# A two-block transformer kernel on one core: dense products of the second block with 512 columns of activations per matmul instead of 256

## The chip, the core and the metric

The kernel runs on one core of a Trainium2 chip. The metric is the device time of one execution in microseconds (us): before the change, the median of three runs is 1532.46 us (1531.75 to 1533.73).

## What is computed

A sequence of 256 tokens of width 1024 passes through a first block (attention, mLSTM, a mixture of experts), which the change does not touch, and then through a second block of two layers. Each layer projects the normed input into several parts, mixes the sequence, attends to 256 memory rows, gates, and projects back. Cut to what matters here:

```python
def second_block(x, mem, ...):
    mem_n = rms_norm_2(mem, mem_norm_w)
    for i in range(2):
        h = rms_norm_2(x, norm_w[i])
        if i == 0:                                   # gated linear attention (GLA)
            q, k, v, r, z, xq = split_cols(h @ gla_w_in, [512, 512, 2048, 16, 3072, 1024])
            ...
        else:                                        # S5
            u, z, xq = split_cols(h @ s5_w_in, [2048, 3072, 1024])
            y = s5_chunked(u, ...) + d * u
            y = jax.nn.gelu(y)
            seq_out = y * jax.nn.sigmoid(y @ w_glu + b_glu)
        xa = memory_attention(xq, mem_n, xa_w_kv[i])  # 4 heads of 256
        y = jnp.concatenate([seq_out, xa], -1) * jax.nn.silu(z)
        x = x + y @ w_out[i]
    return rms_norm_2(x, final_norm_w)
```

## The kernel before

All weights and activations are float32. For the dense products every operand is split on the chip into a high part (rounded to the matmul type fp32r) and a low part (the rest): `split` (L265 to 269) does the high part on ScalarE (L267) and the low part on VectorE (L268), or on GpSimd. `halves` (L271) loads 1 MB of weights into a tile `w` of 128 x 2048 and yields two halves of 1024 columns, each as a pair `whi`, `wlo`. A product is then three matmuls, hi by hi, hi by lo and lo by hi (`mm3`, L282), all issued in `mm` (L280), each with 256 moving columns (the 256 tokens). `dense_t` (L288) makes 256 output features out of one `w`: 2 halves x 8 slices of the contraction x 3, which is 48 matmuls into one PSUM bank; VectorE then multiplies the bank by the row of inverse norms `r` as it copies it out.

Layer one is `gla` (L1395 to 1581). It runs, in the order of the code: `gqk` (4 `dense_t`: queries and keys), a 16-wide gate product, `gv` (values, `dense_n`, eight blocks of 256 columns, tokens as weights), the chunked attention core, then `gx` (4 `dense_t`: the queries of the memory attention, tile `hf`), `mem_attention` (L1141 to 1169), and a loop of 12 `gz` blocks (`dense_t`, evicted as `zt` at L1555, Silu, `gated`), each followed with one block's delay by `wout` (L1378), 48 matmuls into four accumulating banks `acc`. Into the `gz` loop the code writes 8 calls of `s5_out` (L1324, all on GpSimd, with a DMA store of `tab2` at L1343) and 8 of `s5_in` (L1363), which prepare tables for layer two: GpSimd issues two DMA loads (L1367 and L1368, tile `gv`, the second of them from `md`), VectorE does six operations (L1372 to 1374), GpSimd issues the DMA store (L1375). The tile `s_t2` is shared by both and has two buffers, so a table can be begun only when the store of the one before the last has landed. In the profile it is called `s_t`.

`mem_attention` handles four heads one after the other, each in two tiles of 128 queries: scores (tile `at` from `w` and `hf`), maximum (L1154, L1155), exponential (L1158), reciprocal and scaling (L1159, L1160), two transposes (L1162); at the end of a head a copy (L1163), the product with the values (`at` from `xpT` and `w`), and a copy into `hf` (L1168).

Layer two is `s5` (L1584 to 1796): `su` (8 blocks) and `sx` (4 blocks) with the state products between them, then `mem_attention` again, with 12 `z_block` (L1607, evicted at L1610) and a complex scan on VectorE (L1634 to 1637) between its steps, then the output tables, and last the GLU: 16 features `f`, each 48 matmuls from `in_sglu`, a Sigmoid on ScalarE, and `wout`.

The order of each engine's instructions is not that of the code: the tile framework moves instructions across blocks where data and buffers allow. What it cannot move across is a change of the PSUM pools. `psum_banks` (L222) releases the pool of PSUM banks and allocates another with other tags, and a tile of the new pool comes after the tiles of the old one. In `gla` the second pool is `acc=4, ps=2, at=2` banks: the memory attention (`at`), the `gz` blocks (`ps`) and `wout` (`acc`) have banks side by side.

Of the kernel before, what the change touches and what calls it, by code (L numbers as in the profile page):

```python
# [19 lines left out]
T = 256  # L20
# [68 lines left out]
def pack(inputs):  # L89
# [55 lines left out]
    a["gv"] = blocks(np.ascontiguousarray(w[:, 1024:3072]), 256)  # L145
# [62 lines left out]
class Kern:  # L208
# [13 lines left out]
    def psum_banks(self, **banks):  # L222

        if self.ps is not None:
            self.ps.release()
        assert sum(banks.values()) <= 8
# [4 lines left out]
    def psum(self, tag="ps"):  # L231
        return self.ps.tile([128, 512], F32, tag=tag, name=tag, bufs=self.banks[tag])
# [69 lines left out]

    def dense_n(self, src, act):
# [37 lines left out]
    def rows(self, pool, col, name=None):  # L341

        ps = self.psum()[:, :T]
        for t in range(2):
            self.mm(ps[:, 128 * t:128 * t + 128], col[:, t:t + 1].to_broadcast([128, 128]), self.ident, True, True)
        if name is None:
            return ps
        r = self.t(pool, [128, T], name)
        self.nc.scalar.activation(r, ps, AF.Copy)
        return r  # L350
# [1044 lines left out]
    def gla(self):  # L1395
        nc, io, tc = self.nc, self.io, self.tc
        G0 = self.G
        with tc.tile_pool(name="g", bufs=1) as P, tc.tile_pool(name="gw", bufs=2) as W, \
# [10 lines left out]
            hh = self.t(G0, [128, 8, T], "hh", F32R)  # L1409
            hl = self.t(G0, [128, 8, T], "hl", F32R)  # L1410
# [6 lines left out]
            h = (hh, hl)  # L1417
            first = self.dense_t(io["gqk"][0], h)
# [14 lines left out]
            for s in range(2):  # L1433
                o = self.t(P, [128, 4, T], "gqk%d" % s)
                for b in range(2):
                    ps = first if s + b == 0 else self.dense_t(io["gqk"][2 * s + b], h)
                    nc.vector.tensor_mul(o[:, 2 * b:2 * b + 2], ps, bc(r, 2))
                qk.append(o)
# [8 lines left out]
            for k in range(8):  # L1447
                self.mm3(ps, [x[:, k] for x in wrs], [x[:, k] for x in h], k == 0, k == 7)
# [36 lines left out]
            for b in range(8):  # L1485
                ps = self.dense_n(io["gv"][b], h)
                for t in range(2):
                    nc.scalar.activation(v[:, t, 256 * b:256 * b + 256], ps[:, t], AF.Copy, scale=rc[:, t:t + 1])
# [76 lines left out]
            hh = self.t(G0, [128, 8, T], "hh", F32R)  # L1565
            hl = self.t(G0, [128, 8, T], "hl", F32R)
            ps = self.psum("at")[:, :2].rearrange("p (t n) -> p t n", t=2)
# [10 lines left out]
            self.h = (hh, hl)  # L1578
            self.su0 = self.dense_t(io["su"][0], self.h)
# [4 lines left out]
    def s5(self, out):  # L1584
        nc, io, tc = self.nc, self.io, self.tc
        x3 = self.xT
        self.psum_banks(ps=2, st=3, at=3)
        with ExitStack() as S:
# [13 lines left out]
            with ExitStack() as S2:  # L1602
# [4 lines left out]
                def z_block(b):  # L1607
                    ps = self.dense_t(io["sz"][b], h)
                    zt = self.t(W, [128, 2, T], "zt")
                    nc.vector.tensor_mul(zt, ps, bc(r, 2))  # L1610
# [49 lines left out]
                with tc.tile_pool(name="su", bufs=1) as S1:  # L1660
# [47 lines left out]
                    for n in range(4):  # L1708
                        for b in (n, n + 4):
                            ps = self.dense_t(io["su"][b], h, st if 2 * n + b // 4 >= 3 else iter(())) if b else self.su0  # L1710
                            u = self.t(W, [128, 2, T], "zt")
                            nc.vector.tensor_mul(u, ps, bc(r, 2))
# [3 lines left out]
                    for b in range(4):  # L1716
                        ps = self.dense_t(io["sx"][b], h, st)
                        nc.vector.tensor_mul(xa[:, 2 * b:2 * b + 2], ps, bc(r, 2))
# [15 lines left out]
            ys = [[None] * 16, [None] * 16]  # L1734
            for jb in range(8):
# [11 lines left out]
                for par in range(2):  # L1747
# [4 lines left out]
                    for n in range(2):  # L1752
                        ys[n][f] = y2[:, n]
                    self.split(u, ys[0][f], ys[1][f])
# [9 lines left out]
            for f in (16, 17, 18, 19, 20, 21, 22, 23, 0, 1, 2, 3, 4, 5, 6, 7, 8, 9, 10, 11, 12, 13, 14, 15):  # L1764
# [6 lines left out]
                ps = self.psum()[:, :T]  # L1771
# [28 lines left out]
def tile_kernel(ctx: ExitStack, tc: tile.TileContext, io, out, dbg=None, upto=99):  # L1800
# [8 lines left out]
    if upto >= 3:  # L1809
        k.psum_banks(ps=8)  # L1810
# [27 lines left out]
```

## Time and profile before

| | |
|---|---|
| median of three runs | 1532.46 us |
| the profiled execution | 1531.12 us, span 1529.1 us, mean granted TensorE clock 0.919 |
| TensorE (PE) busy | 1349.4 us, 88% |
| VectorE (DVE) busy | 762.3 us, 50% |
| ScalarE (ACT) busy | 551.3 us, 36% |
| GpSimd (POOL) busy | 321.7 us, 21% |
| memory attention of layer one to the end of its `wout` | 910.42 to 1097.00 us |
| `su` and `sx` with the state products | 1112.60 to 1225.46 us |
| memory attention of layer two, z blocks, scan | 1225.46 to 1322.37 us |
| GLU and its `wout` | 1376.49 to 1514.74 us |

Times in the trace are microseconds from the start of the span. PE is busy for most of the span, so stretches in which it is not, and stretches in which another engine is full, are where to look. The granted clock is a share of TensorE's full 2.4 GHz; at 0.50 it is at its lower level of 1.2 GHz.

### The profile page before, as it was taken

The numbers are of one execution on the slowest core, as the hardware profiler recorded it, in microseconds if no ns is written. First come the engines' busy times: TensorE is split into PE (matmuls) and PEld (weight loads), VectorE is DVE, ScalarE is ACT, GpSimd is POOL, SyncE is SP. The second block draws the span as 40 slices with busy tenths as digits, with TensorE's granted clock in tenths as the row PEclk, the third lists the DMA queues.
The fourth block names the chain that finished last, engine by engine and source line by source line (L and its number), as shares of the span: only waits on it lengthen the run. The fifth ranks groups of instructions, "written<-read, shape, count | busy, mean of one in ns | idle before, by whom it ended". The sixth has DMA issues, their size and how long they took to land. (4 is left out here: it accounts for less than half of the span.)

```text
span 1529.1 us, 25802 instructions
## 1 busy us (share of the span) xinstructions
PE 1349.4 (88%) x10632; PEld 1072.4 (70%) x10632; DVE 762.3 (50%) x1498; ACT 551.3 (36%) x861; POOL 321.7 (21%) x450
## 2 busy tenths in 40 slices
PE   5999998888798889776698976899989998999997
PEld 2777896444454545311188976799988998999997
DVE  2766454721243300100177766756735899754553
ACT  3754552221211212110045423454522255444443
POOL 0041031321323231100059765100310000030001
PEclk8999999987898988887798996999989999999998
DMA  9776765999999999999974566755556535574540
GB/s 374 266 267 249 281 230 212 384 397 421 420 408 416 421 420 420 417 421 380 421 264 147 183 183 212 256 196 204 180 181 199 173 111 194 195 214 171 193 139 28
DMA packets 87626, 414.86 MB, mean 271 GB/s; under 512 B 26432, under 2 KB 28016, under 8 KB 43472
## 3 DMA queue, kind: packets, MB, share of 16 engines
q1 hardware_dynamic: 66768, 381.85, 65.7%
q0 software_dynamic: 8016, 22.13, 4.6%
q10 hardware_dynamic: 12720, 9.18, 1.8%
q8 instruction: 86, 1.41, 0.4%
q14 instruction: 36, 0.29, 0.1%
HBM read 392.90 MB, written 20.22 MB: 270 GB/s over the span
## 5 line engine op out<-in xcount | busy, mean ns | idle before, releaser
L267 ACT ACTIVATE whi<-w 128x1024 fp32r<-128x1024 f32 x252 | 263.6, 1055 | 330.4 <-PE ps L280 243.3
L268 DVE TENSOR_TENSOR wlo<-w,whi 128x1024 fp32r<-128x1024 f32 x222 | 275.7, 1245 | 156.8 <-ACT whi L267 156.3
L280 PE MATMUL ps<-hh,whi 128*128 128x256 f32 x928 | 274.3, 296 | 13.3 <-DVE zt L1610 5.0
L280 PE MATMUL ps<-hh,wlo 128*128 128x256 f32 x928 | 269.3, 290 | 5.2 <-DVE wlo L268 5.1
L280 PE MATMUL ps<-hl,whi 128*128 128x256 f32 x928 | 268.4, 289 | 0.9 <-DVE hl L1575 0.7
L280 PEld LDWEIGHTS ps<-hh,whi 128*128 128x128 f32 x928 | 180.7, 195 | 22.0 <-issue 8.7
L280 PEld LDWEIGHTS ps<-hh,wlo 128*128 128x128 f32 x928 | 180.3, 194 | 8.0 <-DVE wlo L268 6.0
L280 PEld LDWEIGHTS ps<-hl,whi 128*128 128x128 f32 x928 | 180.4, 194 | 2.0 <-DVE hl L1575 0.7
L280 PE MATMUL A<-w,xg 128*32 128x512 f32 x984 | 142.8, 681 | 31.1 <-DMA w<-in_w 30.2
L280 PE MATMUL acc<-gyh,whi 128*128 128x256 f32 x384 | 110.6, 288 | 4.0 <-ACT gyh L267 4.0
L280 PE MATMUL acc<-gyl,whi 128*128 128x256 f32 x384 | 111.1, 289 | 1.9 <-DVE gyl L268 1.9
L280 PE MATMUL acc<-gyh,wlo 128*128 128x256 f32 x384 | 109.9, 286 | 0.0
L268 POOL TENSOR_TENSOR wlo<-w,whi 128x1024 fp32r<-128x1024 f32 x30 | 70.7, 2371 | 167.5 <-ACT whi L267 167.4
L934 DVE SCALAR_TENSOR_TENSOR xT<-m,mod,xT 128x256 f32<-128x256 f32 x64 | 27.8, 479 | 140.8 <-PE m L280 140.8
L280 PEld LDWEIGHTS A<-w,xg 128*32 128x32 f32 x984 | 23.9, 114 | 102.1 <-DMA w<-in_w 72.7
L280 PE MATMUL A<-w,gT 128*32 128x512 f32 x512 | 75.4, 690 | 22.3 <-DMA w<-in_w 14.4
L280 PEld LDWEIGHTS acc<-gyh,whi 128*128 128x128 f32 x384 | 74.3, 193 | 4.4 <-ACT gyh L267 4.2
L280 PEld LDWEIGHTS acc<-gyl,whi 128*128 128x128 f32 x384 | 74.4, 194 | 3.1 <-DVE gyl L268 2.4
L280 PEld LDWEIGHTS acc<-gyh,wlo 128*128 128x128 f32 x384 | 74.9, 195 | 0.2 <-issue 0.2
L960 DVE TENSOR_TENSOR g<-g,A 128x512 f32<-128x512 f32 x8 | 5.5, 684 | 134.8 <-PE A L280 134.8
L1755 POOL TENSOR_TENSOR zs<-zs,yy 128x256 f32<-128x256 f32 x16 | 14.0, 893 | 241.3 <-DMA yy<-yd 241.2
L280 PE MATMUL ps<-wlo,hh 128*128 128x256 f32 x192 | 55.7, 290 | 4.6 <-DVE wlo L268 4.6
(585 smaller groups left out, 2768.6 us busy)
## 6 DMA issues: line engine op xcount, KB each, us to landing
w<-in_w SPq DMA_DIRECT2D x187, 1024.0 KB, 11.4
w<-in_wada SPq DMA_DIRECT2D x24, 1024.0 KB, 7.3
w<-in_wo SPq DMA_DIRECT2D x24, 1024.0 KB, 4.9
w<-in_sglu SPq DMA_DIRECT2D x16, 1024.0 KB, 5.0
w<-in_gz SPq DMA_DIRECT2D x12, 1024.0 KB, 5.2
w<-in_sz SPq DMA_DIRECT2D x12, 1024.0 KB, 4.8
w<-in_win SPq DMA_DIRECT2D x10, 1024.0 KB, 7.3
w<-in_xk SPq DMA_DIRECT2D x8, 1024.0 KB, 9.9
```

The lines of the kernel that those rows point to most:

```text
L267: self.nc.scalar.activation(hi, src, AF.Copy)
L268: (eng or self.nc.vector).tensor_sub(lo, src, hi.bitcast(F32))
L280: self.nc.tensor.matmul(ps, l, r, start=start, stop=stop, **kw)
L934: self.nc.vector.scalar_tensor_tensor(self.xT[:, f], pc[:, T * c:T * c + T], self.m(5)[:, f:f + 1], self.xT[:, f], op0=OP.mult, op1=OP.add)
L960: nc.vector.tensor_mul(g1, g1, p3)
L1755: nc.gpsimd.tensor_mul(zs[:, f], zs[:, f], u)
```

## The change

A new `dense_w` takes the place of `dense_t` in 44 blocks (`gqk` 4, `gx` 4, `gz` 12, `su` 8, `sx` 4, `sz` 12). The high and the low half of the activations lie in one tile `h` of `[128, 2, 8, T]`, and one matmul multiplies the high weights by both, 512 columns; a second one of 256 columns multiplies the low weights by the high half. That is 32 matmuls in place of 48. The result has two parts, so the PSUM tile `pd` has two banks; `whole` joins them: ScalarE copies the second part into a tile `lo`, VectorE adds it to the first (L326) and multiplies by `r` (L327), where one VectorE multiplication stood. The GLU does the same with `mm2`, with a ScalarE copy and a VectorE addition more for each feature. The values `gv` come in blocks of 512 columns: 192 matmuls of 512 in place of 384 of 256. The PSUM pools change with the two-bank tiles:

```diff
+    def mm2(self, ps, l, r, start, stop):
+        self.mm(ps, l[0], r, start, False, skip_group_check=True)
+        self.mm(ps[:, 0], l[1], r[:, 0], False, stop, skip_group_check=True)
+
+    def dense_w(self, src, act, other=iter(())):
+        ps = self.psum("pd")
+        for c, w in enumerate(self.halves(src)):
+            w = [x.rearrange("p (k m) -> p k m", k=8) for x in w]
+            for k in range(8):
+                self.mm2(ps[:, c], [x[:, k] for x in w], act[:, :, k], k == 0, k == 7)
...
+    def whole(self, W, dst, ps, r):
+        lo = self.t(W, [128, 2, T], "lo")
+        self.nc.scalar.activation(lo, ps[:, :, 1], AF.Copy)
+        self.nc.vector.tensor_add(dst, ps[:, :, 0], lo)
+        self.nc.vector.tensor_mul(dst, dst, bc(r, 2))
...
# gla
-            self.psum_banks(acc=4, ps=2, at=2)
+            self.psum_banks(pd=2, at=4)
             xa = self.t(P, [128, 8, T], "hf")
             for b in range(4):
-                ps = self.dense_t(io["gx"][b], h)
-                nc.vector.tensor_mul(xa[:, 2 * b:2 * b + 2], ps, bc(r, 2))
+                ps = self.dense_w(io["gx"][b], h)
+                self.whole(W, xa[:, 2 * b:2 * b + 2], ps, r)
             self.mem_attention(W, xa, self.load_kv(0), xa)
             self.out("xa0", xa)
+            self.psum_banks(pd=2, acc=4)
             acc = [self.psum("acc") for _ in range(4)]
             late = []
             for b in range(12):
-                ps = self.dense_t(io["gz"][b], h)
+                ps = self.dense_w(io["gz"][b], h)
...
                 zt = self.t(W, [128, 2, T], "zt")
-                nc.vector.tensor_mul(zt, ps, bc(r, 2))
+                self.whole(W, zt, ps, r)
...
-                u = self.t(G0, [128, T], "u", bufs=4)
+                u = self.t(G0, [128, T], "u", bufs=3)
...
# s5
-        self.psum_banks(ps=2, st=3, at=3)
+        self.psum_banks(pd=2, st=4)
...
                 V = S2.enter_context(tc.tile_pool(name="sv", bufs=2))
+                self.psum_banks(pd=2, at=4)
                 scan(SCAN_FIRST)
...
-                ps = self.psum()[:, :T]
+                ps = self.psum().rearrange("p (a t) -> p a t", a=2)
                 for j, wg in enumerate(self.halves(io["sglu"][f])):
                     for k in range(8):
-                        self.mm3(ps, [x[:, 128 * k:128 * k + 128] for x in wg], [x[8 * (k % 2) + 4 * j + k // 2] for x in ys],
-                                 j + k == 0, j + k == 8)
+                        self.mm2(ps, [x[:, 128 * k:128 * k + 128] for x in wg], ys[8 * (k % 2) + 4 * j + k // 2], j + k == 0, j + k == 8)
                 sg = self.t(W, [128, T], "sg")
-                nc.scalar.activation(sg, ps, AF.Sigmoid, bias=self.v("s5_b_glu_2", f))
+                nc.scalar.activation(sg, ps[:, 1], AF.Copy)
+                nc.vector.tensor_add(sg, ps[:, 0], sg)
+                nc.scalar.activation(sg, sg, AF.Sigmoid, bias=self.v("s5_b_glu_2", f))
```

Two pool switches are new: one in `gla` between `mem_attention` and the `gz` loop, one in `s5` ahead of the second `mem_attention`. The pool at the start of `gla` goes from `ps=8` to `ps=4, pd=2`.

The order of instructions on the engines moves with the pools. On PE, before, the first steps of layer one's memory attention stand like this (`at` is the attention; the `ps` row ahead of it ends the last `gx` block, those behind it are of the first `gz` block, 40 of them between the first scores and the first transposes):

```order
L280 MATMUL ps<-hh,wlo 128x256
L280 MATMUL at<-w,hf 128x256 x2
L280 MATMUL ps<-hh,whi 128x256
L280 MATMUL ps<-hl,whi 128x256
...
L1162 MATMUL at<-c_ident,xp 128x128 x2
L280 MATMUL at<-w,hf 128x256 x2
L280 MATMUL ps<-hh,wlo 128x256
```

On PE, after the change, at the same place (the first two rows are the end of the last `gx` block, the last two the start of the first `gz` block; between them stand four heads of five rows each, and nothing else):

```order
L283 MATMUL pd<-h,whi 128x512
L283 MATMUL pd<-h,wlo 128x256
L283 MATMUL at<-w,hf 128x256 x2
L1188 MATMUL at<-c_ident,xp 128x128 x2
L283 MATMUL at<-w,hf 128x256 x2
L1188 MATMUL at<-c_ident,xp 128x128 x2
L283 MATMUL at<-xpT,w 128x256 x4
...
L283 MATMUL pd<-h,whi 128x512
L283 MATMUL pd<-h,wlo 128x256
```

All `gz` and `wout` matmuls now stand behind the whole memory attention on PE; the first four `gz` blocks and three of the twelve `wout` stood among its steps before.

On DVE, after the change, the end of the same attention (L1398 to 1400 are `s5_in`, `s_t2` its table; L1180 to 1186 the attention's softmax of the last two query tiles; L271 the low half of a `gz` weight):

```order
L1398 TENSOR_TENSOR s_t_9247<-gv 128x8x64
L1399 TENSOR_TENSOR gA<-gv 128x512
L1400 TENSOR_TENSOR s_t_9247<-s_t_9247,gA 128x8x64
L1180 TENSOR_REDUCE xmx<-at 128x1
L1181 TENSOR_SCALAR xmx<-xmx 128x1
L1185 RECIPROCAL xsm<-xsm 128x1
L1186 TENSOR_SCALAR xp<-xp,xsm 128x256
L1180 TENSOR_REDUCE xmx<-at 128x1
L1181 TENSOR_SCALAR xmx<-xmx 128x1
L271 TENSOR_TENSOR wlo<-w,whi 128x1024 x2
L326 TENSOR_TENSOR zt<-pd,lo 128x512
L327 TENSOR_TENSOR zt<-zt,r 128x512
```

`s_t_9247` is the last of the eight `s5_in` tables: all eight stand ahead of the last two query tiles on DVE, as they did before.

On DVE in layer two, after the change, one z block among the scan (L1667 to 1670) and the second memory attention:

```order
L326 TENSOR_TENSOR zt<-pd,lo 128x512
L1667 TENSOR_TENSOR zs<-Xs,pw 128x448
L1668 TENSOR_TENSOR zs<-Xs,pw 128x448
L1669 TENSOR_TENSOR zs<-zs,Xs 128x448
L1185 RECIPROCAL xsm<-xsm 128x1
L327 TENSOR_TENSOR zt<-zt,r_9512 128x512
L1670 TENSOR_TENSOR Xs<-zs 128x2x7x32
```

Where one eviction stood (L1610 before), two operations stand now, with a scan step's operations between them.

## Rows read from the trace of the kernel before

**Rows 1.** The page's busy time of each engine over the whole span.

```profile
PE 1349.4 (88%) x10632; PEld 1072.4 (70%) x10632; DVE 762.3 (50%) x1498; ACT 551.3 (36%) x861; POOL 321.7 (21%) x450
```

**Rows 2.** Busy time by stretch: us, PE, PEld, DVE, ACT, POOL (instructions), clock, DMA, GB/s.

```profile
910.42:999.61 89.19, 67.02 (x418) 62.49 (x417) 58.28 (x105) 39.11 (x59) 33.62 (x63) 0.83 0.71 228
999.61:1097.00 97.39, 97.39 (x819) 97.39 (x817) 59.40 (x77) 48.19 (x64) 1.02 (x3) 1.00 0.58 197
1112.60:1225.46 112.86, 111.44 (x1296) 102.57 (x1297) 66.15 (x106) 26.68 (x29) 2.44 (x3) 0.96 0.59 184
1225.46:1322.37 96.91, 87.89 (x658) 83.95 (x656) 94.26 (x191) 53.94 (x70) 0.00 (x0) 0.98 0.44 154
1376.49:1514.74 138.25, 138.25 (x1155) 138.25 (x1154) 69.40 (x83) 61.50 (x82) 0.93 (x2) 1.00 0.40 138
```

**Rows 3.** The waits of 884 to 1000 us: engine, line, whom for; us, times, longest.

```profile
PE at L1162 <- DVE xp L1160: 13.4, 4, 7.2
DVE s_t L1372 <- DMA tab<-s_t: 10.2, 2, 8.5
DVE s_t L1372 <- DMA gv<-md: 8.2, 2, 6.1
DVE gA L1373 <- DMA gv<-md: 6.2, 2, 5.8
```

**Rows 4.** Timeline of POOL, 896 to 1000 us: start, us, what, and its idle time before.

```profile
942.30 0.59 POOL L1343 DMA_DIRECT2D tab<-s_t  x1 [0.30 <-POOL s_t L1341]
...
950.64 0.53 POOL L1375 DMA_DIRECT2D tab<-s_t  x1 [0.72 <-DVE s_t L1374]
...
968.28 0.53 POOL L1375 DMA_DIRECT2D tab<-s_t  x1 [0.19 <-issue]
...
989.13 0.53 POOL L1375 DMA_DIRECT2D tab<-s_t  x1 [7.55 <-DVE s_t L1374]
```

**Rows 5.** The tile md: its DMA loads at L1368, from issue to landing.

```profile
DMA to landing us min/median/max: 8.3/11.0/14.2
```

**Rows 6.** Two rows of DVE's timeline one behind the other, in the memory attention.

```profile
950.27 0.68 DVE L1555 TENSOR_TENSOR zt<-ps,r 128x512 f32<-128x512 f32 x1
950.87 0.68 DVE L1373 TENSOR_TENSOR gA<-gv 128x512 f32<-128x512 f32 x1
```

**Rows 7.** Timeline of the last query tile of layer one's memory attention, all engines.

```profile
990.88 1.03 PE L280 MATMUL at<-w,hf 128*128 128x256 f32 x4
...
992.79 0.42 DVE L1154 TENSOR_REDUCE xmx<-at 128x1 f32<-128x256 f32 x1
...
993.24 0.15 DVE L1155 TENSOR_SCALAR xmx<-xmx 128x1 f32<-128x1 f32 x1
...
994.88 0.48 ACT L1158 ACTIVATE xp<-at,xmx 128x256 f32<-128x256 f32 x1
995.25 0.19 ACT L1158 ACTIVATION_READ_ACCUMULATOR xp<-at,xmx 128x1 f32 x1
...
995.67 0.35 DVE L1160 TENSOR_SCALAR xp<-xp,xsm 128x256 f32<-128x256 f32 x1
...
996.90 0.58 ACT L1163 ACTIVATE xpT<-at 128x512 f32<-128x512 f32 x1
...
997.56 1.97 PE L280 MATMUL at<-xpT,w 128*128 128x256 f32 x8
```

**Rows 8.** The score matmuls' tile: duration in ns min/median/max, first and last start.

```profile
L280 PE MATMUL at<-w,hf x32: 377/379/635, 910.4 to 991.5; 128*128 128x256 f32 x32
```

**Rows 9.** Busy time in 40 us, one in the attention, one in the GLU.

```profile
920.00:960.00 40.00, 25.70 (x151) 23.76 (x149) 26.51 (x49) 17.00 (x26) 20.93 (x38) 0.74 0.68 216
...
1400.00:1440.00 40.00, 40.00 (x336) 40.00 (x335) 20.55 (x23) 17.31 (x23) 0.00 (x0) 1.00 0.47 162
```

**Rows 10.** DVE's groups by line in 1225.46 to 1322.37: busy us, mean ns, idle.

```profile
L1610 DVE TENSOR_TENSOR zt<-ps,r 128x512 f32<-128x512 f32 x12 | 8.1, 679 | 0.0
```

**Rows 11.** PE's waits in 1225.46 to 1322.37.

```profile
PE ps L280 <- DVE zt L1610: 5.0, 2, 2.7
```

More of the change, by code (lines that the diff above doesn't have):

```diff
@@ L144, in pack @@
     a["gqk"] = tcols(w[:, :1024])
-    a["gv"] = blocks(np.ascontiguousarray(w[:, 1024:3072]), 256)
+    a["gv"] = np.ascontiguousarray(w[:, 1024:3072].reshape(2, 4, 128, 4, 512).transpose(3, 0, 2, 1, 4))
     a["gr"] = blocks(np.ascontiguousarray(w[:, 3072:3088]), 16)
@@ L225, in psum_banks @@
             self.ps.release()
-        assert sum(banks.values()) <= 8
+        assert sum(n * (1 + (tag == "pd")) for tag, n in banks.items()) <= 8
         self.ps = self.tc.alloc_tile_pool(name="ps%d" % self.n, bufs=1, space=bass.MemoryType.PSUM)
@@ L231, in psum @@
     def psum(self, tag="ps"):
+        if tag == "pd":
+            return self.ps.tile([128, 2, 2, T], F32, tag=tag, name=tag, bufs=self.banks[tag])
         return self.ps.tile([128, 512], F32, tag=tag, name=tag, bufs=self.banks[tag])
@@ L301, in steps_t @@
                     yield
+    def mm2(self, ps, l, r, start, stop):
[7 more added lines that the diff above has]
+                self.mm2(ps[:, c], [x[:, k] for x in w], act[:, :, k], k == 0, k == 7)
+                if k % 4 == 3:
+                    next(other, None)
+        return ps
+    def whole(self, W, dst, ps, r):
[3 more added lines that the diff above has]
+        self.nc.vector.tensor_mul(dst, dst, bc(r, 2))
     def dense_n(self, src, act):
@@ L341, in rows @@
     def rows(self, pool, col, name=None):
-        ps = self.psum()[:, :T]
+        ps = (self.psum() if "ps" in self.banks else self.psum("acc"))[:, :T]
         for t in range(2):
@@ L1408, in gla @@
             self.root_table(W)
-            hh = self.t(G0, [128, 8, T], "hh", F32R)
-            hl = self.t(G0, [128, 8, T], "hl", F32R)
+            h = self.t(G0, [128, 2, 8, T], "h", F32R)
+            hh, hl = h[:, 0], h[:, 1]
             ps = self.psum()[:, :4].rearrange("p (t n) -> p t n", t=2)
@@ L1416, in gla @@
                 self.square_sums(G0, k, self.xT[:, k], mg[:, k], ps, bufs=3, eng=nc.vector)
-            h = (hh, hl)
-            first = self.dense_t(io["gqk"][0], h)
+            first = self.dense_w(io["gqk"][0], h)
             r12 = self.t(P, [128, 2, 2], "r12")
@@ L1435, in gla @@
                 for b in range(2):
-                    ps = first if s + b == 0 else self.dense_t(io["gqk"][2 * s + b], h)
-                    nc.vector.tensor_mul(o[:, 2 * b:2 * b + 2], ps, bc(r, 2))
+                    ps = first if s + b == 0 else self.dense_w(io["gqk"][2 * s + b], h)
+                    self.whole(W, o[:, 2 * b:2 * b + 2], ps, r)
                 qk.append(o)
@@ L1447, in gla @@
             for k in range(8):
-                self.mm3(ps, [x[:, k] for x in wrs], [x[:, k] for x in h], k == 0, k == 7)
+                self.mm3(ps, [x[:, k] for x in wrs], [hh[:, k], hl[:, k]], k == 0, k == 7)
             rT = self.t(P, [16, T], "rT")
@@ L1484, in gla @@
             v = self.t(P, [128, 2, 2048], "gv")
-            for b in range(8):
-                ps = self.dense_n(io["gv"][b], h)
+            for b in range(4):
+                ps = [self.psum() for _ in range(2)]
+                for n in range(2):
+                    for i, w in enumerate(self.halves(io["gv"][b, n])):
+                        w = [x.rearrange("p (k m) -> p k m", k=2) for x in w]
+                        for t in range(2):
+                            for k in range(2):
+                                d = 4 * n + 2 * i + k
+                                self.mm3(ps[t], [x[:, d, 128 * t:128 * t + 128] for x in (hh, hl)], [x[:, k] for x in w], d == 0, d == 7)
                 for t in range(2):
-                    nc.scalar.activation(v[:, t, 256 * b:256 * b + 256], ps[:, t], AF.Copy, scale=rc[:, t:t + 1])
+                    nc.scalar.activation(v[:, t, 512 * b:512 * b + 512], ps[t], AF.Copy, scale=rc[:, t:t + 1])
             for k in range(8):
@@ L1563, in gla @@
                         self.mark = self.last
[L1565 to L1567 removed]
+            h = self.t(G0, [128, 2, 8, T], "h", F32R)
+            hh, hl = h[:, 0], h[:, 1]
+            ps = self.psum("pd").rearrange("p a b t -> p (a b t)")[:, :2].rearrange("p (t n) -> p t n", t=2)
             for k in range(8):
                 src = acc[k // 2][:, T * (k % 2):T * (k % 2) + T].rearrange("p (c s) -> p s c", s=4)
[L1570 removed]
+                u = self.t(G0, [128, T], "u", bufs=3)
                 nc.vector.tensor_add(u.rearrange("p (s c) -> p s c", s=4), src,
@@ L1577, in gla @@
                 nc.gpsimd.tensor_copy(self.xT[:, k], u)
-            self.h = (hh, hl)
-            self.su0 = self.dense_t(io["su"][0], self.h)
+            self.h = h
+            self.su0 = self.dense_w(io["su"][0], self.h)
             self.r = self.rows(G0, self.inv_root(G0, ps[:, :, 0], "rc3"), "r3")
@@ L1607, in z_block @@
                 def z_block(b):
-                    ps = self.dense_t(io["sz"][b], h)
+                    ps = self.dense_w(io["sz"][b], h)
                     zt = self.t(W, [128, 2, T], "zt")
-                    nc.vector.tensor_mul(zt, ps, bc(r, 2))
+                    self.whole(W, zt, ps, r)
                     if b < 8:
@@ L1709, in s5 @@
                         for b in (n, n + 4):
-                            ps = self.dense_t(io["su"][b], h, st if 2 * n + b // 4 >= 3 else iter(())) if b else self.su0
+                            ps = self.dense_w(io["su"][b], h, st if 2 * n + b // 4 >= 3 else iter(())) if b else self.su0
                             u = self.t(W, [128, 2, T], "zt")
-                            nc.vector.tensor_mul(u, ps, bc(r, 2))
+                            self.whole(W, u, ps, r)
                             for a in range(2):
@@ L1716, in s5 @@
                     for b in range(4):
-                        ps = self.dense_t(io["sx"][b], h, st)
-                        nc.vector.tensor_mul(xa[:, 2 * b:2 * b + 2], ps, bc(r, 2))
+                        ps = self.dense_w(io["sx"][b], h, st)
+                        self.whole(W, xa[:, 2 * b:2 * b + 2], ps, r)
                     for _ in st:
@@ L1733, in s5 @@
             W = S.enter_context(tc.tile_pool(name="sgw", bufs=2))
-            ys = [[None] * 16, [None] * 16]
+            ys = [None] * 16
             for jb in range(8):
@@ L1751, in s5 @@
                     y2 = self.t(P, [128, 2, T], "U", F32R, bufs=8) if par else self.t(Y, [128, 2, T], "y%d" % jb, F32R)
-                    for n in range(2):
-                        ys[n][f] = y2[:, n]
-                    self.split(u, ys[0][f], ys[1][f])
+                    ys[f] = y2
+                    self.split(u, y2[:, 0], y2[:, 1])
                     nc.gpsimd.tensor_mul(zs[:, f], zs[:, f], u)
@@ L1809, in tile_kernel @@
     if upto >= 3:
-        k.psum_banks(ps=8)
+        k.psum_banks(ps=4, pd=2)
         k.gla()
```

1 line of the change is left out of this document (removed).

## The prediction, made before the change was run

> **What bounds the kernel now.** I read the page's busy times first, then the busy time by stretch of the second block, then inside the one stretch where no engine is full its waits and timelines. The page says that PE is busy for 88% of the span [rows 1]. The stretches say where that is not so [rows 2]. In the end of layer one (999.61 to 1097.00), in `su` and `sx`, and in the GLU, PE is busy throughout or nearly: there fewer or shorter matmuls pay in full. In layer two's memory attention with the z blocks (1225.46 to 1322.37) DVE is busy 94.26 of 96.91 us and PE 87.89: there a DVE operation more costs its length, and a shorter matmul nothing. In layer one's memory attention (910.42 to 999.61) nothing is full: PE 67.02 of 89.19 us, DVE 58.28, and the clock is 0.83. The reader should see there what sets the pace: PE waits 13.4 us for the softmax's last step, and DVE waits 24.6 us (10.2, 8.2, 6.2) for the table DMAs of `s5_out` and `s5_in` [rows 3], in whose order on DVE the softmax stands. So this stretch is a chain through DVE, GpSimd and DMA, and the 418 matmul records that PE has in it ride along: 80 are the attention's (each of its 32 float32 matmuls leaves two records, and 16 are transposes), the other 338 are four `gz` blocks (4 x 48 = 192) and three `wout` (3 x 48 = 144), 336 by the code.
>
> **The price of a matmul.** Where PE is full, 336 matmuls of 256 columns fill 40.00 us [rows 9], 119.0 ns each from start to start; 819 in 97.39 us [rows 2] is the same. The GLU has 1155 in 138.25, 119.7 ns. 256 columns at 2.4 GHz are 106.7 ns, so some 12.4 ns of each are not columns. No row shows a lone fp32r matmul of 512 columns. The upper end is two of 256, 238 ns. The lower end is the float32 matmul of 256 columns, each of whose two records is a pass that takes the time of 512 columns: four score passes last 1.03 us, the last one 0.379, so (1.03 - 0.379) / 3 = 217 ns [rows 7, 8]. I take 226, two paces less one surplus of 12.4, since one instruction of two goes; both rows are about equally near. A pair (512 and 256) then costs 226 + 119 = 345 ns where three cost 357: 12 ns gained of each pair, 13 in the GLU. The Trainium skill, TensorE: Matmul & The Clock Gate, section Back-to-back issue gap, has a gap of columns over the clock plus 2.5 ns: 109 ns for 256 columns and 216 for 512. This case's rows do not agree for 256 columns (119.0); by the page alone a pair would gain only 2.5 ns, and with its 216 beside the measured 119 it would gain 22.
>
> **The change, part by part.**
>
> *The pool switch in layer one.* The order on PE shows that all `gz` and `wout` matmuls stand behind the whole attention, because their banks now come from a pool that is allocated after it. The 336 matmuls that filled the waits of the stretch run after it instead: 336 x 0.119 = 40.0 us are moved from the shade of the chain onto the path. Against that the attention may end sooner. How soon is the main unknown.
>
> The chain is that of the tables. On DVE all eight `s5_in` still stand ahead of the last two query tiles, and on GpSimd `s5_out` and `s5_in` still take turns. Before, the last `tab2` store is issued at 942.30, and the `tab1` stores of the fourth, sixth and eighth table follow at 950.64, 968.28 and 989.13 [rows 4]: 8.3, 17.6 and 20.9 us. The two later steps are each a load that can only be issued behind a store, 0.6 us of issue and 11.0 us to land [rows 5], then six DVE operations of 0.60 (the start of one to the next [rows 6]): 15.2 us at the least. What they have above that is DVE's waiting for attention steps that PE reached late behind dense products, and this goes. So the last table is stored at 950.6 + 2 x 15.2 = 981.0. Then come the last two query tiles. One has 0.42 + 0.15 + 0.48 + 0.19 + 0.15 + 0.35 = 1.7 us of softmax, 2.1 with transposes and handoffs; the next has 1.0 of scores ahead, 3.1; the head's end has 0.58 of copy and 1.97 of values [rows 7], 2.6. That is 7.8, and `gz` starts at 989 instead of 999.6: 10.6 us sooner. Bounds: as late as before, 999.6, if the table chain has nothing to gain; and the attention's own chain, if the tables do not hold it. By the same sums that is 2 x 3.1 + 3.0 = 9.2 us a head, 12.5 if PE is at its lower clock and passes last twice as long, 37 to 50 for four. `gx` ended at 910.4 before and ends some 3 us sooner, by the shorter `gqk` and `gv` ahead of it (64 pairs x 12 ns = 0.8, and 192 x 12 = 2.3 plus handoffs), so at 907: the end is at 944 to 957.
>
> PE is then idle for most of the attention. The clock was already 0.74 in 920 to 960 with PE busy 25.70 of 40 us [rows 9]; with the dense work gone I expect its lower level, 0.50, for most of the stretch. That costs about 1.5 us at the start of `gz` until the clock is back, and up to 3 in the tail, which I leave to the range. The `gz` blocks behind it gain 12 x 16 x 12 ns = 2.3 us, since PE alone bounds them: a `gz` block with its `wout` is 5.5 + 5.7 = 11.2 us of PE, and DVE's added operation of 0.60 and ScalarE's copy of 0.6 stay far under that (DVE 59.40, ACT 48.19 of 97.39 [rows 2]). Sum of the stretch: 40.0 - 10.6 - 2.3 + 1.5 = **+28.6 us**. What `gqk` and `gv` gain is hidden in the table chain, and counted at nothing.
>
> *su and sx.* PE is busy 111.44 of 112.86 us [rows 2]; 12 blocks x 16 pairs x 12 ns = **-2.3**. The evictions' extra operations lie beside it, DVE being at 66.15.
>
> *z blocks.* The 2.3 us that PE gains are hidden, DVE being full. DVE gets an addition for each of 12 blocks: the eviction lasts 0.679 by its row [rows 10], 0.60 start to start [rows 6], 12 x 0.60 = 7.2. DVE's 2.65 us of idle time could take some of it; on the other hand PE waits 5.0 us for these evictions [rows 11], and the new way is longer by a ScalarE copy of 0.6 each time. I take **+7**, 4.6 to 9 for the range.
>
> *GLU.* 16 x 16 = 256 pairs x (3 x 119.7 - 226 - 119.7 = 13.4 ns) = **-3.4**. The copy and addition more are hidden by the `wout` of the feature before, 24 matmuls or 2.9 us; if that cover falls short at the last feature it costs about 0.5.
>
> *The rest:* the banks at the start (`ps` 8 to 4) and `u` with three buffers in place of four: within 1 us either way, as there PE still has four banks and each `u` lives through three short operations.
>
> **Sum.** 1531.1 (the profiled execution) + 28.6 - 2.3 + 7 - 3.4 = 1561.0. That execution is 1.3 us under the median of the runs, so I forecast 1562.
>
> **Rivals.**
> *A, the other side: the tables do not hold the attention.* If GpSimd and the DMAs run ahead once PE's and DVE's `gz` work is out of their way, the attention ends by its own chain. It decides at T, the start of `gz`: each microsecond of T is one of the result, and below T of 960 or so the change breaks even. At 957 the stretch is 40.0 - 42.6 - 2.3 + 1.5 = -3.4 and the total 1530; at 944 it is 1517; the middle is 1524. For it: DVE's waits for DMA are 24.6 us, and DMA landing may shorten. Against it: the stores at 942 to 989 are serial by buffers, and 31 us of them lie behind 950.
> *B, a 512-column matmul costs two of 256.* Then no pair gains: 2.3 + 2.3 + 3.4 = 8 us more, 1570. For it: nothing shows that the surplus is per instruction. Against it: the score passes at 217.
> *C, the z stage is not lengthened*, the scan moving into DVE's gaps: 1555. Against it: DVE at 94.26 of 96.91.
> *D, the 512-column matmul loses the surplus altogether* (217 ns): 9 ns more on each of 640 pairs, 5.8 us, 1556. The page named above has this as its 216.
>
> **How the numbers follow.** Forecast 0.65, A 0.09, B 0.08, C 0.09, D 0.09. About 0.2%, 3 us, is what a measurement here can tell from no change: faster is below 1529.4, slower above 1535.5. Only A lies there: I give it 0.07 faster and 0.02 same, and 0.01 of same to a sum of all small errors; slower 0.90. The range: T from 977 (12 less) to 999.6 (10.6 more) moves 1562 to 1550 and 1573; with D's 5.8 it reaches 1544, with the z stage's 2 more and part of the tail at the lower clock 1577. It holds B, C and D and leaves out A.
>
> **What would show it right or wrong.** Right: on PE, `at` steps with nothing between them from about 907 to 989, PE busy under a quarter there, the clock near 0.50; the last `tab1` store near 981; `gz` and `wout` without a gap for 135 us, ending near 1126; matmuls of 512 columns at 226 ns; DVE full in a z stage some 7 us longer; the GLU 3.4 us shorter. Wrong: `gz` starting near 950 (A), dense matmuls among the attention's steps, or a DVE idle in the z stage (C).

## The result, and the profile after the change

The change made the kernel slower: the median is 1588.94 us against 1533.1 of the kernel before, a ratio of 1.0362 (95% interval 1.0339 to 1.0386). The forecast of 1562 had the direction right and half of the size. The profiled execution took 1589.6 us, span 1587.5, clock 0.902.

The busy time by stretch, after the change, cut at the same events as [rows 2]; the third row, the norm between the layers, was not shown of before. Columns as there: us, PE, PEld, DVE, ACT, POOL, clock, DMA, GB/s.

```profile
918.27:999.25 80.98, 31.59 (x83) 20.75 (x81) 34.28 (x73) 12.12 (x27) 31.03 (x62) 0.60 0.55 164
999.25:1136.39 137.14, 136.89 (x960) 128.19 (x961) 90.96 (x122) 71.84 (x100) 1.02 (x3) 1.00 0.53 187
1136.39:1157.13 20.74, 14.13 (x70) 11.85 (x69) 12.77 (x20) 10.15 (x20) 16.17 (x28) 0.75 0.30 111
1157.13:1268.18 111.05, 104.69 (x1120) 87.59 (x1120) 73.38 (x121) 32.59 (x41) 0.00 (x0) 0.98 0.62 194
1268.18:1381.30 113.12, 94.13 (x464) 78.44 (x464) 103.20 (x202) 61.64 (x83) 0.00 (x0) 0.89 0.36 132
1436.50:1573.20 136.70, 136.70 (x899) 124.59 (x898) 74.94 (x99) 66.50 (x98) 0.93 (x2) 1.00 0.39 139
```

And the norm of before:

```profile
1097.00:1112.60 15.60, 11.99 (x87) 11.39 (x85) 12.57 (x19) 9.53 (x19) 14.95 (x26) 0.87 0.46 155
```

Layer one's attention now keeps PE busy for 31.59 of 81 us at a clock of 0.60, and the end of layer one lies at 1136.39 where it lay at 1097.00: 39.4 us later. 2.8 of these were there before anything that the change touches (the first product of layer one started at 775.85 instead of 773.02; that start lay between 773.0 and 783.7 in the profiles of this case). The other 36.6 are the change's, where 28.6 were forecast. The norm takes 5.1 us more (0 forecast), `su` and `sx` 1.8 less (2.3), the stretch of the second attention and the z blocks 16.2 more (7), the step to the GLU 1.1 more, the GLU to the end 1.6 less (3.4). That is 58.4, the difference of the two spans.

The end of the attention on PE after the change, in its timeline (start, us, what; in brackets the idle time before it):

```profile
981.34 0.69 PE L1188 MATMUL at<-c_ident,xp 128*128 128x128 f32 x2 [5.45 <-DVE xp L1186]
982.77 3.78 PE L283 MATMUL at<-xpT,w 128*128 128x256 f32 x8 [0.75 <-ACT xpT L1189]
986.35 1.91 PE L283 MATMUL at<-w,hf 128*128 128x256 f32 x4
990.15 0.44 PE L1188 MATMUL at<-c_ident,xp 128*128 128x128 f32 x2 [1.89 <-DVE xp L1186]
990.42 1.03 PE L283 MATMUL at<-w,hf 128*128 128x256 f32 x4
993.35 0.69 PE L1188 MATMUL at<-c_ident,xp 128*128 128x128 f32 x2 [1.89 <-DVE xp L1186]
994.78 3.78 PE L283 MATMUL at<-xpT,w 128*128 128x256 f32 x8 [0.75 <-ACT xpT L1189]
999.25 0.50 PE L283 MATMUL pd<-h,whi 128*128 128x512 f32 x1 [0.69 <-ACT hf L1194]
999.59 0.28 PE L283 MATMUL pd<-h,wlo 128*128 128x256 f32 x1
999.70 0.39 PE L283 MATMUL pd<-h,whi 128*128 128x512 f32 x1
999.93 0.28 PE L283 MATMUL pd<-h,wlo 128*128 128x256 f32 x1
```

The value product takes 3.78 us where [rows 7] has 1.97: the granted clock is 0.50 from 982.77 to 986.30, and again from 994.78 to 998.50. Here too is the price of the new pair: from 999.70 to 999.93 the 512 columns, 0.23 us, and some 0.12 to the next matmul at 1000.05.

POOL's timeline has the stores of the last two tables:

```profile
976.26 0.56 POOL L1401 DMA_DIRECT2D tab<-s_t  x1 [5.77 <-DVE s_t L1400]
984.11 0.53 POOL L1401 DMA_DIRECT2D tab<-s_t  x1 [7.29 <-DVE s_t L1400]
```

### The profile page after: what moved, and what is told of

It is laid out like the page before. It is cut to its first block, busy times and chain, and to the rows that moved or that the text cites. A ratio compares the mean times of both kernels' runs of the same rounds, so it can differ in the third digit from the quotient of the medians.

```text
span 1587.5 us, 23631 instructions
## 1 busy us (share of the span) xinstructions
PE 1358.2 (86%) x9480; PEld 1016.7 (64%) x9480; DVE 799.7 (50%) x1558; ACT 569.3 (36%) x907; POOL 325.3 (20%) x450
## 5 line engine op out<-in xcount | busy, mean ns | idle before, releaser
L271 DVE TENSOR_TENSOR wlo<-w,whi 128x1024 fp32r<-128x1024 f32 x222 | 276.5, 1249 | 148.7 <-ACT whi L270 148.3
L283 PE MATMUL pd<-h,whi 128*128 128x512 f32 x704 | 265.8, 414 | 9.5 <-DVE zt L326 4.6
L283 PE MATMUL pd<-h,wlo 128*128 128x256 f32 x704 | 205.4, 293 | 6.8 <-DVE wlo L271 6.8
L283 PEld LDWEIGHTS pd<-h,whi 128*128 128x128 f32 x704 | 137.9, 196 | 43.6 <-DVE hf L326 3.3
L283 PEld LDWEIGHTS pd<-h,wlo 128*128 128x128 f32 x704 | 138.2, 196 | 8.9 <-DVE wlo L271 8.2
L271 POOL TENSOR_TENSOR wlo<-w,whi 128x1024 fp32r<-128x1024 f32 x30 | 70.6, 2368 | 167.7 <-ACT whi L270 167.6
L283 PE MATMUL ps<-hh,whi 128*128 128x256 f32 x224 | 65.8, 294 | 0.8 <-ACT hh L270 0.8
L283 PE MATMUL ps<-hl,whi 128*128 128x256 f32 x224 | 64.4, 288 | 0.3 <-DVE hl L271 0.3
L283 PE MATMUL ps<-hh,wlo 128*128 128x256 f32 x224 | 64.2, 287 | 0.0
```

The costliest lines, as they stand in the source:

```text
L271: (eng or self.nc.vector).tensor_sub(lo, src, hi.bitcast(F32))
L283: self.nc.tensor.matmul(ps, l, r, start=start, stop=stop, **kw)
```

## The experiments

Each was timed beside the kernel before (medians 1531.8 to 1534.0 in the five sets), and not beside the changed kernel (the one after the change): a difference from that one is between two sets, and comes out 1 to 4 us smaller by the ratios than by the medians, which the text gives.

**switch_gla: the second pool alone.** The kernel before with

```diff
-            self.psum_banks(acc=4, ps=2, at=2)
+            self.psum_banks(ps=4, at=4)
...
             self.mem_attention(W, xa, self.load_kv(0), xa)
+            self.psum_banks(ps=4, acc=4)
```

> The kernel before, with 256-column matmuls and one-operation evictions everywhere, but layer one's second half in two PSUM pools (ps=4, at=4, then ps=4, acc=4) as the change has it. Theory S (the new pool alone puts the 336 gz and wout matmuls behind the attention): about 40 us moved onto the path, less 0 to 3 that the attention ends sooner, so 1569 to 1573 us; PE between the end of gx and the start of gz shows only attention steps, clock near 0.6. Rival W (the loss in layer one comes from the wide matmuls and the longer evictions): 1533 to 1543.

Measured: 1564.08 us, ratio 1.0232 (1.0203 to 1.0261), +32. PE's order from `gx` to `gz` is that of the changed kernel, with no wide matmul in it. Its stretches:

```profile
912.04:994.00 81.96, 30.66 (x82) 20.26 (x80) 37.02 (x75) 11.15 (x26) 32.79 (x66) 0.60 0.59 178
994.90:1132.20 137.30, 137.30 (x1152) 137.30 (x1151) 83.81 (x110) 66.04 (x88) 0.97 (x3) 1.00 0.54 186
```

All 12 x 96 = 1152 dense matmuls now stand in the second row, where [rows 2] has 819. Theory S stands and W falls; the size is a little under what was expected, as the attention took 82.9 us from the first scores to the start of `gz`, 6.3 less than in [rows 2], where 0 to 3 less were expected.

**wide_no_switch: the changed kernel in one pool.** `psum_banks(acc=4, pd=1, at=2)`, no second switch.

> The changed kernel, wide matmuls everywhere, but layer one's second half in one pool again (acc=4, one two-bank pd, at=2), so that gz and wout may stand among the attention's steps. Theory S: most of the 37 us of layer one come back; one pd instead of two costs an eviction's 2 us now and then, so 1552 to 1562. Rival W: within 5 us of the changed kernel, 1584 to 1594.

Measured: 1568.99, ratio 1.025 (1.0221 to 1.028): 20 us came back, fewer than expected. In its profile PE waits 7.4 us for the evictions of the single `pd` (the wait list of 916 to 1126):

```profile
PE pd L283 <- DVE hf L326: 4.4, 2, 2.4
PE pd L283 <- DVE zt L326: 3.0, 1, 3.0
```

That left open whether the pool was all of it:

**after_gla_narrow: layer one's second half undone.** `gx`, `gz` and the first `su` block as before, in the old pool.

```diff
-            self.psum_banks(pd=2, at=4)
+            self.psum_banks(acc=4, ps=2, at=2)
...
-            self.psum_banks(pd=2, acc=4)
...
-                ps = self.dense_w(io["gz"][b], h)
+                ps = self.dense_t(io["gz"][b], (hh, hl))
```

> The changed kernel with layer one's second half as before: gx, gz and the first su block by three 256-column matmuls and one eviction operation, in one pool (acc=4, ps=2, at=2). Theory S (the second pool costs what it cost alone, 32 us): 1554 to 1559 us. Rival (it costs less beside the other parts, as the one-pool kernel with a single pd, which gave back 20, might suggest): 1566 to 1571, and then the single pd was not what kept 12 us there.

Measured: 1555.3, ratio 1.0159 (1.0132 to 1.0186), 33.6 under the changed kernel (31 by the ratios). Put in alone the switch costs 32; taken out, together with the wide form of these blocks, it gives about as much. So the 13 us that wide_no_switch kept belong to its own way, a single `pd` or the wide form in one pool; these two were not parted, though the waits above, which this run's profile does not have, speak for the single `pd`.

**switch_s5: layer two's pool switch alone.** `psum_banks(ps=4, st=4)`, and `psum_banks(ps=4, at=4)` ahead of the second attention, in the kernel before.

> The kernel before, but layer two in two pools (ps=4, st=4, then ps=4, at=4 ahead of the second memory attention), nothing else changed. Theory S5 (the pool change empties PE between sx and the second attention, as the changed kernel's 14.1 us for its last 46 sx matmuls suggest): 5 to 10 us slower, 1538 to 1543. Rival D (what layer two loses comes from the added VectorE operations alone): 1531 to 1535.

Measured: 1530.01, ratio 0.9986 (0.9966 to 1.0006): it costs nothing that can be told, and theory S5 falls. The z blocks still find the new pool's banks free in time and stand among the attention's steps.

**z_two_ops: the longer eviction alone,** in the 12 z blocks of the kernel before:

```diff
-                    nc.vector.tensor_mul(zt, ps, bc(r, 2))
+                    lo = self.t(W, [128, 2, T], "lo")
+                    nc.scalar.activation(lo, ps, AF.Copy)
+                    nc.vector.tensor_tensor(zt, ps, lo, op=OP.max)
+                    nc.vector.tensor_mul(zt, zt, bc(r, 2))
```

> The kernel before, but each of the 12 z blocks is evicted as in the change: a ScalarE copy of the bank, a VectorE operation of bank and copy (a maximum, so the value stays), then the multiplication by r. Theory D (VectorE is full in that stretch): 12 x 0.60 = 7 us slower, 1538 to 1542, the stretch from the first second-attention scores to the last z block 104 us instead of 96.9. Rival S5: under 2 us, 1531 to 1535.

Measured: 1546.38, ratio 1.0104 (1.0079 to 1.013), +14.6: the cause that theory D named, at twice its price. The stretch, and PE's waits in it:

```profile
1237.00:1347.52 110.52, 91.69 (x659) 86.98 (x657) 103.98 (x205) 62.86 (x84) 0.00 (x0) 0.92 0.39 142
```

```profile
PE ps L280 <- DVE wlo L268: 7.6, 3, 3.2
PE at L1162 <- DVE xp L1160: 5.5, 3, 2.5
PE st L280 <- DVE zt L1612: 3.0, 1, 3.0
PE ps L280 <- DVE zt L1612: 1.9, 1, 1.9
```

In the kernel before, PE waited there for weights only once, and for no softmax:

```profile
PE ps L280 <- DVE wlo L268: 1.6, 1, 1.6
```

DVE's own waits in the stretch of z_two_ops:

```profile
DVE xmx L1154 <- PE at L280: 2.9, 4, 1.8
DVE wlo L268 <- ACT whi L267: 1.6, 1, 1.6
DVE zt L1612 <- ACT lo L1611: 1.4, 1, 1.4
```

DVE has 9.7 us more work than [rows 2], and is idle for 6.5 us instead of 2.7. PE now waits 13.1 us for weights and softmax that come late from DVE (7.6 and 5.5), and the clock is 0.92 instead of 0.98. DVE waits in turn: 2.9 us for attention steps on PE, where it waited 1.9 before, and 3.0 for ScalarE, for high halves and for the new copy. What the copy and the VectorE operation cost singly was not parted. (The profiled execution took 1557.85 us; its layer one started 10.7 us late, which the stretch does not hold.)

**after_z_narrow: the reverse.** The changed kernel, the z blocks by `dense_t` and one multiplication, pool `ps=4, at=4`.

> The changed kernel with the 12 z blocks of layer two by three 256-column matmuls and one eviction operation again (pool ps=4, at=4). Theory D (the added ScalarE copy and VectorE addition cost this stretch 14 us, as the same two operations did when they were put into the kernel before): 1572 to 1578 us. Rival (the stretch is longer for the new pool or the order): within 4 us of the changed kernel.

Measured: 1576.69, ratio 1.0294 (1.027 to 1.0318), 12.3 under the changed kernel (10 by the ratios), as D expects, though the pool's banks were changed with it (`ps=4` for two two-bank `pd`).

**u_three: the third part.** In the kernel before, `u` with `bufs=3` instead of 4, nothing else.

> The kernel before with three buffers in place of four for the tile u of the norm between the two layers, as the change has it, nothing else. Theory U (the third buffer is given back late, by GpSimd's copies, which stand behind its scan powers): the stretch from the last output matmul of layer one to the end of the norm takes 20.9 us instead of 15.7, as in every kernel here with three buffers, and the kernel 4 to 5 us more, 1536 to 1538. Rival (the two-bank pd there is what lengthens it): 15.7 us in that stretch, 1530 to 1534.

Measured: 1539.22, ratio 1.0033 (1.0014 to 1.0052), +5.2, as theory U says. DVE's timeline in the norm has a wait of 3.08 us there, for a copy on GpSimd that gives the buffer back:

```profile
1113.62 0.61 DVE L1571 TENSOR_TENSOR u<-acc,xT 128x256 f32<-128x256 f32 x1 [3.08 <-POOL xT L1577]
```

The copies stand on POOL between the powers for the scan; with four buffers DVE does not meet them.

**after_su_narrow: su and sx undone** (three matmuls and one multiplication, in the first bank of `pd`).

> The changed kernel with su and sx by three 256-column matmuls and one eviction operation again (in the first bank of pd). If the wide form costs this stretch what the landmarks suggest (131.8 us from the end of layer one to the second attention, against 128.6 before): 3 to 6 us faster than the changed kernel, 1583 to 1586. Rival (the stretch differs by chance or by the work that VectorE takes over from it): within 2 us of the changed kernel.

Measured: 1580.96, ratio 1.0338 (1.0299 to 1.0377). The interval overlaps that of the changed kernel (8 us under it by the medians, 4 by the ratios), so this one is inconclusive.

**glu_only: the part that should pay.** The kernel before with the GLU's two `mm2` hunks alone.

> The kernel before with the GLU's products alone made wide (512 and 256 columns, ScalarE copy and VectorE addition before the Sigmoid). Theory P (a matmul's time goes by its columns, 236 ns for 512 as the changed kernel's GLU shows): a pair costs 353 ns where three cost 359, 256 x 6 ns = 1.5 us faster, 0.1%, hardly to be told from no change. Rival Q (the saving of 12 to 13 ns a pair that the prediction took): 3.4 us faster.

Measured: 1530.6, ratio 0.9983 (0.9967 to 0.9999), 1.8 us faster. This is nearest P's size, but the interval, 0.2 to 5 us, holds Q as well. The changed kernel's GLU row tells them apart: of 136.70 us, 384 `wout` matmuls at 119.7 ns are 46.0, and 90.7 over 256 pairs is 354 ns, where three cost 359.

**tables_late and after_tables_late: what holds the attention.** The tables are started behind a GpSimd copy that reads the attention's last output:

```diff
+            gate = nc.gpsimd.tensor_copy(mg[:, 2:3, 0], xa[:, 7, 0:1])
...
-                    with tc.issue_after(start.ins):
+                    with tc.issue_after(gate.ins):
                         if b == 4:
```

> The kernel before, but the eight s5_in tables are begun only when the memory attention of layer one is done (their GpSimd loads stand behind a copy that reads the attention's output), so they lie in the gz loop. Theory T (the table DMAs hold the attention's steps on VectorE, 24.6 us of DMA waits): the attention with its 336 dense matmuls ends 10 to 20 us sooner, gz after it is PE-bound as before, so 1512 to 1522 us. Rival A (the attention's own chain sets the stretch): 1529 to 1534. A third outcome, VectorE too full in the gz loop (59 + 29 of 97 us): slower than 1536.

> The changed kernel with the same move of the tables. Theory T: with nothing else on VectorE the attention runs by its own chain, 9.2 to 12.5 us a head, so gz starts at 955 to 968 instead of 999 and the kernel takes 1545 to 1558 us. Rival A: gz starts within 5 us of 999 and the time stays at 1584 to 1592.

Measured: 1534.95, ratio 1.0023 (1.0006 to 1.004), and 1593.74, ratio 1.041 (1.0384 to 1.0436). Neither became faster, and both missed theory T's times; tables_late lies a microsecond above rival A's, after_tables_late above both. And yet the attention did what theory T said. In tables_late it took 46.5 us from the first scores to its last copy into `hf`, where the kernel before took 89.8. On PE in after_tables_late the value products of the four heads start so:

```profile
922.52 3.78 PE L283 MATMUL at<-xpT,w 128*128 128x256 f32 x8 [0.69 <-ACT xpT L1189]
...
934.47 3.78 PE L283 MATMUL at<-xpT,w 128*128 128x256 f32 x8 [0.69 <-ACT xpT L1189]
...
946.28 3.78 PE L283 MATMUL at<-xpT,w 128*128 128x256 f32 x8 [0.75 <-ACT xpT L1189]
...
958.28 3.78 PE L283 MATMUL at<-xpT,w 128*128 128x256 f32 x8 [0.75 <-ACT xpT L1189]
...
962.75 0.50 PE L283 MATMUL pd<-h,whi 128*128 128x512 f32 x1 [0.69 <-ACT hf L1194]
```

12.0 us a head, the chain at a mean granted clock of 0.66, and `gz` at 962.75 instead of 999.25. The gain was lost again behind it. The tables' DMA waits now stand in VectorE's order in the `gz` loop, and PE waits there for the low halves (the wait list of 960 to 1160):

```profile
PE acc L283 <- DVE gyl L271: 21.6, 6, 9.9
DVE s_t L1398 <- DMA tab<-s_t: 15.7, 4, 6.1
DVE s_t L1398 <- DMA gv<-md: 10.5, 2, 7.4
```

In tables_late's loop, too, VectorE waits 21.1 us for table stores, and PE 19.6 us for low halves of weights. So the wait was moved, not removed. The next runs take the tables off VectorE:

**tables_pool and three more.** One line of `s5_in` in the kernel before:

```diff
-        e = self.nc.vector
+        e = self.nc.gpsimd
```

> The kernel before with the six operations of each s5_in table on GpSimd instead of VectorE, nothing else. Theory T (the attention of layer one is held by table DMAs only because the table's operations stand in VectorE's order): attention and the gz loop become PE-bound throughout, 67.0 + 97.4 = 164.4 us of PE work from the first scores against 186.6, so the end of gz comes up to 22 us sooner, 1511 to 1518 us. Rival: GpSimd is too slow for the tables (some 9 us each) and they are late for layer two, or its work slows VectorE: 1528 or more.

Measured: 1513.33 us, ratio 0.9864 (0.9844 to 0.9885): 19 us faster than the kernel before. The attention and the blocks among it are PE-bound now:

```profile
910.38:957.57 47.19, 45.71 (x323) 42.56 (x322) 36.36 (x60) 32.13 (x50) 40.41 (x55) 1.00 0.66 216
957.57:1043.60 86.03, 86.03 (x721) 86.00 (x720) 67.05 (x64) 39.66 (x51) 62.56 (x63) 1.00 0.68 221
```

47.19 us where [rows 2] has 89.19, though with 323 matmul records instead of 418, at a clock of 1.00. In this profile, of the slowest of the five executions (1524.0; the others took 1508.6 to 1514.5), 23.6 us were lost afterwards:

```profile
PE ps L280 <- ACT whi L267: 23.6, 1, 23.6
```

The load of the last `gz` weights stands on the sync queue (issued at 1065.48) behind loads of layer two, which came only when the last table had been stored (1061.0).

> The same with the GLU's wide products added. The two lie in different stretches and should add: 1.5 us under tables_pool, 1509 to 1516 us.

Measured: 1518.17, ratio 0.9899 (0.9863 to 0.9936); the intervals overlap, so whether the GLU adds there can't be told.

> The changed kernel with the tables' operations on GpSimd. Theory T: the attention runs by its own chain as it did with the tables moved behind it (12.0 us a head, gz at 962 instead of 999), and now nothing in the gz loop waits for tables, so some 37 us less than the changed kernel, 1550 to 1556 us. Rival: gz is bound by something else after the attention too, 1575 or more.

Measured: 1571.15, ratio 1.0255 (1.0229 to 1.028), 17.8 under the changed kernel and not 37. `gz` started at 976.2, since PE had waits left for the softmax, the longest of 10.4 us in the first head, and `gz` had waits of its own behind. Behind the 10.4 us stands a single VectorE operation, the scaling of a softmax, which takes 0.35 to 0.37 us in the changed kernel. It ended when GpSimd, after 11 us of table operations one behind the other, issued its next DMAs:

```profile
921.47 8.91 DVE L1186 TENSOR_SCALAR xp<-xp,xsm 128x256 f32<-128x256 f32 x1
930.18 0.58 POOL L1401 DMA_DIRECT2D tab<-s_t  x1
```

So the rival named for tables_pool, that GpSimd's work slows VectorE, holds in part. All five profiles with the tables on GpSimd have VectorE operations of 2.8 us or more (up to 12.2, in tables_pool_mark_glu); none of the other 13 has one above 2.6. Why VectorE takes so long there was not tested.

For the weights' wait, the mark that loads of layer two stand behind was moved (`if b == 10` to `if b == 11`):

> The kernel before with the tables on GpSimd, and the loads for layer two issued on the sync queue only behind the last output weights of layer one (the mark moved from block 10 to block 11). In the profile of tables_pool the last gz load stands behind a load that waits for the last table, and PE waits 23.6 us for it. If that wait is the only thing behind it: up to 20 us under tables_pool, 1493 to 1503 us. Rival (the weights are late for another reason, or layer two then starts late by as much): 1508 to 1514.

> The same with the GLU's wide products: 1.5 us less than tables_pool_mark if the two add, within what can be told.

Measured: 1515.86, ratio 0.989 (0.986 to 0.9919), and 1510.26, ratio 0.9865 (0.984 to 0.989). The mark gained nothing that can be told: in its profile the 23.6 us became 13.2 at the next place, where the last output product waits for a ScalarE operation that stands behind layer two's first weights. That is the rival's first case, the weights late for another reason, though 1515.86 lies outside both ranges. Those weights were loaded when the table chain on GpSimd had ended, at 1065. In the profile of tables_pool_mark_glu, its fastest execution (1506.15), PE has no such wait. The fastest versions are tables_pool and tables_pool_mark_glu, which can't be told apart.

## Why the prediction was right in sign and wrong in size

*The pool switch, +28.6: right in mechanism, too small by 8.0.* The 336 matmuls are on the path, and the table chain holds the attention as worked out: the last store came at 984.1, and without the 2.8 us of a late start at 981.3, where 981.0 was forecast. (Some luck is in this: the last two steps took 14.3 and 14.8 us, less than the 15.2 "at the least", and the fourth store came 1.6 later than reckoned, the late start aside.) The step that failed is the tail behind it: 7.8 us were reckoned, it was 15.1 (984.11 to 999.25). I counted two query tiles and one head's end. But the third head's last softmax steps stand among the last table's operations on VectorE, so PE was still in that head's values when the table was stored (982.77 to 986.5), and the fourth head's first scores stand behind them: nearly a whole head. And the passes took some 0.43 us each instead of 0.217, all but those of the last scores at 990.42: the granted clock was 0.50 in the values and the first scores, 1.00 in the last scores. That clock I had named and left to the range. `gz` thus began no sooner than before: the bound of 999.6, which I had as the worst case. The 1.5 us for a slow start of `gz` rested on no row, and no run shows them: the clock was 1.00 from 999.25 on. The stretch of `gz` took 0.2 us less than 97.39 + 40.0, where its pairs were to give 2.3. In the terms of the sum: 40.0 - 3.2 - 0.2 = 36.6 (the late start taken off) instead of 40.0 - 10.6 - 2.3 + 1.5 = 28.6.

*z blocks, +7: right in mechanism, less than half the size, and the largest miss, 9.2 us.* DVE's own work grew by 8.9 us (7.2 forecast). The other 7.3 are idle time of DVE, 9.9 us instead of 2.65, which the sum had at nothing. As in z_two_ops, the full DVE is late for PE, and DVE waits in turn: in the changed kernel 4.1 us for attention steps on PE (1.9 before), and 5.6 for ScalarE, 2.3 for an exponential, 1.7 for the new copy, 1.6 for high halves. An engine with 2.65 us to spare in 97 does not only get longer by what is added.

*"The rest: within 1 us": wrong.* `u` with three buffers cost 5. "Three short operations" overlooked that the last of them, a GpSimd copy, stands behind other work on its queue. The start of layer one was not free either: `gx` started 3.2 us later than before, after the 2.8, though it was to start 3 sooner. PE waits there 5.9 us for operations of the attention core ahead of it (3.7 on ScalarE, 2.2 on VectorE) where it waited 1.0 and not at all; this would fit the fewer banks (`ps` 8 to 4), but no run has these alone. The table chain hid this, as it was to hide the gain.

*The pair, 345 ns: 351 to 354.* A matmul of 512 columns takes 230 to 236 ns, near rival B's 238 and far from D's 217: over the 213 ns of 512 columns at 2.4 GHz that is a surplus of 17 to 23 ns, where 12.4 would go by instruction and 24.8 by column. Of 3.4 us in the GLU 1.6 came. The figure of the Trainium skill that I set beside the rows (TensorE: Matmul & The Clock Gate, Back-to-back issue gap; 216 ns, which the page gives for an isolated matmul, as the prediction did not say) is further off here than the row of two 256-column matmuls.

*su and sx, -2.3:* 1.8 in the two profiles. After_su_narrow does not confirm it, and it stays open.

*The rivals.* A asked whether the tables hold the attention. They do, and in the change they went on doing so; once freed in after_tables_late the attention took 50 us, the upper end of its reckoned 37 to 50, at 12.0 us a head. (The 9.2 a head at full clock counts the head's end as 3.0, where the tail has 2.6.) But A's "each microsecond of T is one of the result" did not hold there: `gz` started 36.5 us sooner and the kernel was no faster. C was wrong.

By medians, the parts that were put in alone are 32.3 + 14.6 + 5.2 - 1.8 = 50.3 of the 55.8 us; the other 5.5 were put to no part.

## What to carry to other kernels

A change of pools can be a change of order: in layer one the work that had filled an earlier stretch's waits came to stand behind that stretch, and most of its length was added (32 of 40 us); in layer two, where the order stayed (switch_s5), the new pool cost nothing that can be told. Before buying fewer matmul instructions, look up what a column costs in a full stretch, and what the added eviction costs on the engine that is full there. Work that waits for DMA in the middle of a busy engine's order holds everything behind it: moving it in time moved the wait, moving it to an engine with room, here by one line, gave 19 us, though single VectorE operations beside it then took many times their length, and PE waited for them.

## What the runs showed of the hardware that was not expected

The wide matmul saved almost nothing by its size: 512 columns in 230 to 236 ns, two of 256 in 238 to 239. A VectorE operation of 0.6 us, put 12 times into a stretch where VectorE was 97% busy, cost the kernel 14.6 us with its ScalarE copy, 1.2 us each. A softmax scaling of 0.35 us on VectorE took 8.91 while GpSimd ran the table operations one behind the other (after_tables_pool); the cause is open.
